# A hybrid decoder layer on one core: weight rows of 512 columns and four accumulators from the second merge branch on

## The chip, the cores and the metric

The kernel runs on one core of one Trainium2 chip. The metric is the device time of one execution in microseconds; the median of three runs is given, and beside it one execution that the hardware profiler recorded.

## The reference

One inference step of a one-layer decoder trunk in float32, for 256 prompt tokens and 8 x 4 sample tokens, T = 288 tokens together, with a model width of 2048.

```python
h = rmsnorm(x, norm_mix)
P = h @ w_in                       # (288 x 2048) @ (2048 x 16416)
y[0], y[1], y[2] = retention(P), gated_deltanet(P), gla(P)      # 1024 wide each
br    = einsum('blnc,ncd->blnd', y, w_branch)                   # three times (1024 x 2048)
gates = sigmoid(mg + b_merge)      # mg: the last 3 * 2048 columns of P
x = x + sum(gates * br, axis=2) @ w_o                           # 2048 x 2048
gate, up = split(rmsnorm(x, norm_ffn) @ w_gate_up, 2)           # 2048 x (2 * 5632)
x = x + (silu(gate) * up) @ w_down                              # 5632 x 2048
y = rmsnorm(x, norm_final)         # and the new states of the three mixers
```

## The kernel before

Activations are kept transposed, 128 channels on the partitions and 288 tokens along the free axis, so a weight block of 128 x 128 is TensorE's stationary operand and the tokens stream past it. Each float32 operand is split into a high part (`xh`, `yh`, `ah`, `m0`; for weights `wh`) and the rest (`xl`, `yl`, `al`, `m1`; `wl`), and a product is the sum of three matmuls: high by high, low activations by high weights, high activations by low weights.

All large products go through `dense` and `products` (lines 324 and 330). One call makes 256 output columns: two accumulators of [128, 288] in two PSUM banks of the pool `pd` (four banks; another four, `pm`, serve the mixers and the transposes). The contraction runs in blocks of 128 rows (k). `load` (line 318) fetches four of them at a time, [128, 4, 256], 512 KB, through SP's DMA queue; the pool `raw` holds four such loads. Two k at a time are split: ACT casts `wh` (line 347), DVE subtracts to get `wl` (line 348, recorded as L131); there are four buffers of each. Then 2 x 2 x 3 matmuls follow (recorded as L125).

The order of work: setup; the mixers, whose projections by `x_in` are interleaved with the mixers' own steps; then three merge branches, `branch(n, order)` (line 1219); `merge_out` (line 1259) with `w_o`; `ffn` (line 1307). A branch loads the eight blocks of its mixer's result from DRAM (`yr` from `ys`, line 1225, two buffers) and splits them into `yh` and `yl` (ACT at L169, DVE at L131). Then it goes over eight groups j of 256 columns. A group first makes the gate logits from columns 10272 + 2048 n + 256 j of `w_in` (16 k, eviction `evg`), then the branch product from `w_branch` (8 k, eviction `evb`). Branch 0 stores its gated product in DRAM (`accd`). Branch 1 loads it again, one `yr` tile for each 128 columns (line 1248), and adds. Branch 2 adds and hands on the split sum `m0`, `m1` (`merged`). `merge_out` loads the residual (`xres` from `xT`, line 1271, three buffers), and starts the first gate product of the feed-forward part early. `ffn` goes over two halves of 22 blocks of 128 hidden columns: for each 256 of them a gate and an up product (16 k each), then eight down products over 22 k. After each of the last eight, the rows are transposed by TensorE (L122), squared by ACT and multiplied by the final norm's gain by DVE.

A Tile scheduler decides the order on each engine's queue; what `tc.high_priority()` encloses (the weight loads and splits) comes early. Queues are in order: an instruction that waits holds up what stands behind it.

Of the kernel before, what the change touches and what calls it, by code (L numbers as in the profile page):

```python
# [10 lines left out]
F32 = mybir.dt.float32  # L11
# [3 lines left out]
ALU = mybir.AluOpType  # L15
# [14 lines left out]
HALF = FFB // 2  # L30
# [24 lines left out]
def shape_consts():  # L55
    """Tables that depend on shapes and positions alone."""
# [42 lines left out]
class Trunk:  # L99
    def __init__(self, ctx, tc, ins, outs):  # L100
        self.ctx, self.tc, self.nc = ctx, tc, tc.nc
        self.i, self.o = ins, outs
        self.uid = 0
        self.active = []

# [50 lines left out]
    def pump(self, part=None):  # L156
        """Emits the next steps of the mixers under way."""
# [15 lines left out]
    def setup(self):  # L173
# [41 lines left out]
        # keeps the tensor engine busy until x is there, for its clock  # L215
# [83 lines left out]
    def rms(self, pool, ssq, tag):  # L299
        """ssq [tokens, group, part] of partial sums of squares -> 1/rms [tokens, group]."""  # L300
# [7 lines left out]
    def rowscale(self, pool, r, tag):  # L308
        """r [tokens, group] on every partition, [P, T]."""
# [63 lines left out]
    def gates(self):  # L373
# [21 lines left out]
        # running sums over time of log-sigmoid of the forget logits  # L395
# [7 lines left out]
    def gate_cols(self, z, bz):  # L403
        """Decay sums and write strengths of the delta rule, by head rows and by token columns."""
# [74 lines left out]
    def gdn_conv(self, pair, part):  # L479
        """One of q, k, v of a pair of heads: projection, convolution, 2*silu -> [P, 2, T]."""  # L480
# [50 lines left out]
    def gated(self, n, c0):  # L531
        """2*silu of a projection of 256 columns -> [P, 2, T]."""
# [11 lines left out]
    def finish(self, tr_ps, gate, gcol, n, blk):  # L544
        """y = transposed output * gate (* gain), kept in DRAM until the branch product."""
# [7 lines left out]
    def gdn_mix(self, pair, qs, ks, vs, szs):  # L553
# [12 lines left out]
        for z in hd:  # L566
            # norms of q and k per token, token-major k and v with their factors
# [40 lines left out]
        # chains of the two heads: prompt chunks [P, 4, P] as (chunk, head), samples [NS, 2, NS]  # L608
# [3 lines left out]
        for hh, z in enumerate(hd):  # L612
            # decays, k k^T and k q^T
# [31 lines left out]
        # inverses of the unit triangular systems (u: transposed) by doubling of the block size: up to 8 with a  # L645
        # block in each partition, up to 32 by the diagonal blocks of 32
# [56 lines left out]
        # blocks of 64  # L703
# [23 lines left out]
        # the whole blocks  # L727
# [16 lines left out]
        # outputs and states  # L744
# [84 lines left out]
    # outer products of the sample states: rows hi, hi, lo of k against hi, lo, hi of v  # L829
# [22 lines left out]
    def diag8(self, t, wide, thin):  # L852
        """Pairs of [72, 8, 8] (heads and chunks by 16 blocks, heads of the samples by 4) and the scratch."""
# [9 lines left out]
    def gdn_setup(self):  # L863
# [7 lines left out]
        # scratch of the diagonal blocks of 8; the second pair stays 0 beside them  # L871
# [20 lines left out]
    def values(self, v):  # L892
        """v: [P, 2, T] of one head -> token-major [P, 2, 256] and [NS, 256]."""
# [128 lines left out]
    def spread(self, h, q, f):  # L1022
        """q * f of the samples, high and low part, masked per batch: [P, NB, 2 NS]."""
# [80 lines left out]
    def gla_logits(self, pair):  # L1104
        """The forget logits of two heads: min(z, 0) and exp(-|z|), [P, 2, T] each."""
# [14 lines left out]
    def gla_head(self, h, q, k, v, sg, b):  # L1120
# [16 lines left out]
        for n, s in enumerate(LEVELS + (128,)):  # L1137
# [18 lines left out]
            if s >= 32:  # L1156
                # only the blocks of the level
# [18 lines left out]
        # decayed q and k of the states  # L1176
# [42 lines left out]
    def branch(self, n, order, emit=None):  # L1219
# [11 lines left out]
        for j in range(D // CHUNK):  # L1231
            th = [self.t(self.bp, (P, T), "bt", bufs=4) for _ in range(2)]

            def evg(m, pp):
                blk = n * KT + 2 * j + m
# [3 lines left out]
            self.x_in(O_MG + n * D + j * CHUNK, evg)  # L1239

            def evb(m, pp):
                k = 2 * j + m
# [11 lines left out]
            self.dense(yh, yl, wb[:, :, j * CHUNK:(j + 1) * CHUNK], 8, evb)  # L1254
# [4 lines left out]
    def merge_out(self, merged, bp):  # L1259
        """x + merged @ w_o, its norm's split operands and 1/rms rows."""  # L1260
# [6 lines left out]
        for j in range(D // CHUNK):  # L1267
            def ev(m, pp):
                k = 2 * j + m
# [14 lines left out]
            self.dense([z[0] for z in merged], [z[1] for z in merged], wo[:, :, j * CHUNK:(j + 1) * CHUNK], KT, ev)  # L1284
# [20 lines left out]
        self.early = self.products(blocks(xh), blocks(xl), wg[:, :, 0:CHUNK], KT, False, norm())  # L1305

    def ffn(self, st):
# [5 lines left out]
        NJ = D // CHUNK  # L1313
# [4 lines left out]
        for half in range(2):  # L1318
# [24 lines left out]
            for j in range(NJ):  # L1343
# [5 lines left out]
                if half == 0:  # L1349
                    continue  # L1350
# [102 lines left out]
```

## Time and profile before

| | us |
|---|---|
| median of three runs (lowest, highest) | 2365.64 (2364.16, 2368.34) |
| span of the profiled execution | 2364.7 |
| median less that span | 0.9 |
| TensorE busy in the span | 2206.0 (93%) |
| VectorE busy | 1363.7 (58%) |
| ScalarE busy | 1023.4 (43%) |
| DMA, mean over the span | 157 GB/s |

The page's first part gives the busy time of each engine, its second the same in 40 slices of the span. Matrix records overlap, since each lasts about 0.3 us while a new one starts every 0.13 us; so the pace of TensorE is read from counts of records in a stretch and not from their durations. In a table by stretches the columns are: the stretch in us from the span's start, its length, then busy time and number of instructions of PE (matmuls), PEld (weight loads), DVE, ACT and POOL, the mean granted TensorE clock (1.00 is 2.4 GHz, 0.50 would be 1.2), the mean busy share of the 16 DMA engines, and GB/s. Records are counted in each stretch that they touch. In the list of waits the columns are who waited for whom, us in total, times, longest. In the chain each row is a start, a duration and what ran or was waited for.

### The profile page before, as it was taken

What the parts mean: (1) busy time and instruction counts of PE and PEld (TensorE: products, weight loads), DVE (VectorE), ACT (ScalarE), POOL (GpSimd) and SP (SyncE); (2) the same over time, 40 slices, a digit from 0 to 9 for tenths busy, and PEclk for the clock granted to TensorE, in tenths of its full rate; (3) what the DMA queues carried; (4) which work ended last, traced back from release to release, by engine and by line L of the source; (5) the groups of instructions that cost most, each with busy time, mean ns of one, the idle gap of its engine ahead of it and who ended that gap; (6) DMA issues with size and microseconds to landing.
All of it is one profiled execution on the core that took longest, in us unless ns stands there. A gap on an engine that the chain in (4) does not pass through costs nothing.

```text
span 2364.7 us, 42849 instructions
## 1 busy us (share of the span) xinstructions
PE 2206.0 (93%) x16476; PEld 2139.8 (90%) x16476; DVE 1363.7 (58%) x2952; ACT 1023.4 (43%) x2138; POOL 209.1 (9%) x264
## 2 busy tenths in 40 slices
PE   8686998996899899989989999999999999999997
PEld 6676898996799899989989999999999999999997
DVE  4554685684478566445445466655555455655554
ACT  4352453453256345334334344444444344444443
POOL 2000230231044124000000000000000000000000
PEclk8797998998899999999999999999999999999999
DMA  8986576588667776888887776655555555555553
GB/s 170 111 113 115 138 195 139 133 160 142 110 142 170 157 157 173 187 149 193 159 148 167 139 179 187 189 162 168 164 167 161 169 168 163 169 162 169 156 159 127
DMA packets 387609, 371.74 MB, mean 157 GB/s; under 512 B 26370, under 2 KB 384860, under 8 KB 387244
## 3 DMA queue, kind: packets, MB, share of 16 engines
q1 hardware_dynamic: 386236, 366.22, 65.9%
q8 instruction: 129, 2.11, 0.4%
q0 software_dynamic: 896, 2.45, 0.3%
q14 instruction: 76, 0.62, 0.1%
q10 hardware_dynamic: 272, 0.34, 0.1%
HBM read 342.02 MB, written 26.92 MB: 156 GB/s over the span
## 4 chain that ended last, share of the span: by engine, by line
PE 75%; DMA 15%; DVE 4%; SPq 2%; ACT 2%; issue 1%; POOL 1%; DVEq 0%; POOLq 0%; ACTq 0%
PE pd L125 69%; DMA raw<-in_w_in_dram 6%; PE pm L125 5%; DMA yr<-ys 2%; DVE wl L131 2%; DMA dgu<-u 1%; PE pm L122 1%; DMA dgb<-bt 1%; DMA srow<-in_state_gdn_conv_dram 1%; DMA s<-in_state_ret_dram 1%; DMA out_dram<-s 1%; ACT wh L347 1%; DMA uc<-dgu 1%; DMA b<-dgbs 1%; DVE r L140 0%
## 5 line engine op out<-in xcount | busy, mean ns | idle before, releaser
L131 DVE TENSOR_TENSOR wl<-raw,wh 128x512 fp32r<-128x512 f32 (+1 forms) x1208 | 847.4, 705 | 788.9 <-ACT wh L347 763.6
L347 ACT CAST wh<-raw 128x512 fp32r<-128x512 f32 x1200 | 738.1, 619 | 1050.8 <-PE pd L125 855.2
L125 PE MATMUL pd<-xh,wh 128*128 128x288 f32 x3472 | 1049.3, 303 | 60.4 <-ACT wh L347 55.8
L125 PE MATMUL pd<-xh,wl 128*128 128x288 f32 x3472 | 1048.3, 304 | 34.7 <-DVE wl L131 34.7
L125 PE MATMUL pd<-xl,wh 128*128 128x288 f32 x3472 | 1048.4, 302 | 0.2 <-DVE xl L140 0.2
L125 PEld LDWEIGHTS pd<-xh,wh 128*128 128x128 f32 x3472 | 671.0, 194 | 69.6 <-ACT wh L347 60.6
L125 PEld LDWEIGHTS pd<-xh,wl 128*128 128x128 f32 x3472 | 669.1, 193 | 44.2 <-DVE wl L131 40.5
L125 PEld LDWEIGHTS pd<-xl,wh 128*128 128x128 f32 x3472 | 670.5, 193 | 3.6 <-issue 1.0
L125 PE MATMUL pd<-ah,wl 128*128 128x288 f32 x704 | 208.0, 295 | 0.0
L125 PE MATMUL pd<-al,wh 128*128 128x288 f32 x704 | 207.8, 295 | 0.0
L125 PE MATMUL pd<-ah,wh 128*128 128x288 f32 x704 | 207.8, 295 | 0.0
L125 PEld LDWEIGHTS pd<-ah,wh 128*128 128x128 f32 x704 | 132.5, 188 | 0.1
L125 PEld LDWEIGHTS pd<-ah,wl 128*128 128x128 f32 x704 | 132.3, 188 | 0.0
L125 PEld LDWEIGHTS pd<-al,wh 128*128 128x128 f32 x704 | 132.1, 188 | 0.0
L125 PE MATMUL pd<-yh,wh 128*128 128x288 f32 x384 | 113.4, 298 | 4.3 <-ACT wh L347 2.8
L125 PE MATMUL pd<-yl,wh 128*128 128x288 f32 x384 | 114.4, 298 | 0.3 <-DVE yl L131 0.3
L125 PE MATMUL pd<-yh,wl 128*128 128x288 f32 x384 | 114.0, 297 | 0.0
L125 PE MATMUL pd<-m,wh 128*128 128x288 f32 x512 | 101.6, 295 | 0.0
L125 PEld LDWEIGHTS pd<-m,wh 128*128 128x128 f32 x512 | 82.1, 188 | 0.0
L125 PEld LDWEIGHTS pd<-yh,wh 128*128 128x128 f32 x384 | 72.5, 190 | 5.6 <-ACT wh L347 3.0
L125 PE MATMUL pd<-m,wl 128*128 128x288 f32 x256 | 75.5, 295 | 0.0
L145 POOL TENSOR_TENSOR fr<-fs,c_mh 128x3 f32<-128x3 f32 x1 | 0.8, 849 | 843.1 <-DVE fs L137 843.1
(336 smaller groups left out, 1827.6 us busy)
## 6 DMA issues: line engine op xcount, KB each, us to landing
raw<-in_w_in_dram SPq DMA_DIRECT2D x252, 512.0 KB
raw<-in_w_gate_up_dram SPq DMA_DIRECT2D x176, 512.0 KB
raw<-in_w_down_dram SPq DMA_DIRECT2D x80, 512.0 KB
raw<-in_w_branch_dram SPq DMA_DIRECT2D x48, 512.0 KB
raw<-in_w_o_dram SPq DMA_DIRECT2D x32, 512.0 KB
out_dram<-s SPq DMA_DIRECT2D x16, 512.0 KB
s<-in_state_gdn_dram SPq DMA_DIRECT2D x8, 512.0 KB
s<-in_state_ret_dram SPq DMA_DIRECT2D x16, 256.0 KB
```

Of the source, the lines that this page charges most:

```text
L122: self.nc.tensor.transpose(out, in_, self.ident[:k, :k])
L125: self.nc.tensor.matmul(out, lhsT=lhsT, rhs=rhs, start=start, stop=stop)
L131: self.nc.vector.tensor_tensor(out, a, b, op=op)
L145: self.nc.gpsimd.tensor_tensor(out, in_, c[:n].to_broadcast(list(in_.shape)), op=ALU.pow)
L347: nc.scalar.copy(h, src)
```

## The change

From branch 1 on, products go through two new functions, `wide` and `products4`: 512 output columns in a call, four accumulators, taken in turn from `pd` and `pm` (four banks each). A load holds two k of 512 columns, [128, 2, 512], the same 512 KB in rows of 2 KB in place of 1 KB; a split handles one k of 512 columns, the same 128 x 512 elements. Mixers and branch 0 keep `dense`. The tiles `bt` get eight buffers, `sg` one of twice the size. The feed-forward part goes over 24 and 20 hidden blocks in place of 22 and 22. The final transposes go to banks of the pool whose group was just emptied, one [128, 512] tile for each group of tokens.

```diff
-HALF = FFB // 2
+PARTS = (24, 20)
+WIDE = 512
...
+    def wide(self, xh, xl, wv, kt, evict):
+        acc, self.early = self.early or self.products4(xh, xl, wv, kt), None
+        pool, tiles = acc
+        for m in range(4):
+            evict(m, tiles[m][:, :T])
+        return pool
+
+    def products4(self, xh, xl, wv, kt, steps=None):
+        nc, tc = self.nc, self.tc
+        pool, tag = ((self.pd, "pd"), (self.pm, "pm"))[self.turn]
+        self.turn = 1 - self.turn
+        acc = [self.t(pool, (P, 512), tag) for _ in range(4)]
+        for k0 in range(0, kt, 2):
+            raw = self.t(self.wp, (P, 2, WIDE), "raw", bufs=4)
+            with tc.high_priority():
+                nc.sync.dma_start(out=raw, in_=wv[:, k0:k0 + 2])
+            for k in range(2):
+                wh = self.t(self.wp, (P, WIDE), "wh", F32R, bufs=4)
+                wl = self.t(self.wp, (P, WIDE), "wl", F32R, bufs=4)
+                with tc.high_priority():
+                    nc.scalar.copy(wh, raw[:, k])
+                    self.tt(wl, raw[:, k], wh.bitcast(F32), ALU.subtract)
+                kk = k0 + k
+                for m in range(4):
+                    ms = slice(m * P, (m + 1) * P)
+                    o = acc[m][:, :T]
+                    self.mm(o, wh[:, ms], xh[kk], kk == 0, False)
+                    self.mm(o, wh[:, ms], xl[kk], False, False)
+                    self.mm(o, wl[:, ms], xh[kk], False, kk == kt - 1)
+            if steps is not None:
+                next(steps)
+        return (pool, tag), acc
...
     def branch(self, n, order, emit=None):
...
-        for j in range(D // CHUNK):
-            th = [self.t(self.bp, (P, T), "bt", bufs=4) for _ in range(2)]
+        W = WIDE if n else CHUNK
+        for j in range(D // W):
+            th = [self.t(self.bp, (P, T), "bt", bufs=8) for _ in range(W // P)]
...
-            self.x_in(O_MG + n * D + j * CHUNK, evg)
+            if n:
+                self.wide(blocks(self.xh), blocks(self.xl), self.w_in(O_MG + n * D + j * W, W), KT, evg)
+            else:
+                self.x_in(O_MG + j * W, evg)
...
-            self.dense(yh, yl, wb[:, :, j * CHUNK:(j + 1) * CHUNK], 8, evb)
+            (self.wide if n else self.dense)(yh, yl, wb[:, :, j * W:(j + 1) * W], 8, evb)
...
     def merge_out(self, merged, bp):
...
-            self.dense([z[0] for z in merged], [z[1] for z in merged], wo[:, :, j * CHUNK:(j + 1) * CHUNK], KT, ev)
+            self.wide([z[0] for z in merged], [z[1] for z in merged], wo[:, :, j * WIDE:(j + 1) * WIDE], KT, ev)
...
     def ffn(self, st):
...
+        b0 = 0
+        for part in PARTS:
             ah, al = [], []
+            for j in range(part // 4):
+                c0 = (b0 + 4 * j) * P
+                sg = self.t(fp, (P, 4, T), "sg", bufs=1)
...
+                pool, tag = self.wide(ah, al, wd[:, b0:b0 + part, j * WIDE:(j + 1) * WIDE], part, evd)
...
                 for g, (t0, w) in enumerate(GROUPS):
-                    src = pa[:, g * CHUNK:(g + 1) * CHUNK] if g < 2 else pb[:NS, :CHUNK]
-                    junk = self.t(fp, (P, CHUNK), "junk", bufs=2)
+                    src = self.t(pool, (P, 512), tag)[:w]
+                    for m in range(4):
+                        self.tr(src[:, m * P:(m + 1) * P], self.x2[4 * j + m][:, t0:t0 + w])
+                    junk = self.t(fp, (P, WIDE), "junk", bufs=2)
                     self.act(junk[:w], src, AF.Square, accum_out=ssq[:w, g, j:j + 1])
                     self.tt(xo[g][:, cs], src, nfb[:w, cs], ALU.mult)
```

Up to branch 1 all queues hold the same instructions in the same order. ACT's queue at the entry of branch 1, after the last evictions of branch 0's gate logits (`bt`), stood before as

```order
L347 CAST wh_12449<-raw_12447 128x512
L169 CAST yh_12403<-yr_12401 128x288
L347 CAST wh_12465<-raw_12447 128x512
L347 CAST wh_12483<-raw_12481 128x512
L169 CAST yh_12409<-yr_12407 128x288
L169 CAST yh_12415<-yr_12413 128x288
L347 CAST wh_12499<-raw_12481 128x512
L347 CAST wh_12517<-raw_12515 128x512
L169 CAST yh_12421<-yr_12419 128x288
L169 CAST yh_12427<-yr_12425 128x288
```

and stands now as

```order
L348 CAST wh_12453<-raw_12451 128x512
L171 CAST yh_12403<-yr_12401 128x288
L348 CAST wh_12469<-raw_12451 128x512
L348 CAST wh_12487<-raw_12485 128x512
L171 CAST yh_12409<-yr_12407 128x288
L171 CAST yh_12415<-yr_12413 128x288
L348 CAST wh_12503<-raw_12485 128x512
L171 CAST yh_12421<-yr_12419 128x288
L171 CAST yh_12427<-yr_12425 128x288
L348 CAST wh_12521<-raw_12519 128x512
```

The casts of the branch's own tiles (`yh`) still stand between those of the first gate weights (`wh`); one weight cast fewer lies between the second and the third pair. A weight cast serves 12 matmuls before and after.

SP's queue at the entry of branch 2 stood before as (`accd` tiles of branch 1's last group, `ys` tiles of branch 2, gate loads from `w_in`)

```order
L1248 DMA yr_14216<-accd_108 128x288
L321 DMA raw_14276<-in_w_in_dram 128x4x256
L321 DMA raw_14310<-in_w_in_dram 128x4x256
L321 DMA raw_14344<-in_w_in_dram 128x4x256
L321 DMA raw_14378<-in_w_in_dram 128x4x256
L321 DMA raw_14418<-in_w_branch_dram 128x4x256
L1225 DMA yr_14224<-ys_107 128x288
L321 DMA raw_14452<-in_w_branch_dram 128x4x256
L1225 DMA yr_14230<-ys_107 128x288
L1225 DMA yr_14236<-ys_107 128x288
```

and stands now as

```order
L343 DMA raw_14382<-in_w_in_dram 128x2x512
L343 DMA raw_14416<-in_w_in_dram 128x2x512
L1289 DMA yr_14212<-accd_108 128x288
L1289 DMA yr_14216<-accd_108 128x288
L343 DMA raw_14450<-in_w_in_dram 128x2x512
L1262 DMA yr_14224<-ys_107 128x288
L1262 DMA yr_14230<-ys_107 128x288
L343 DMA raw_14484<-in_w_in_dram 128x2x512
L1262 DMA yr_14236<-ys_107 128x288
L343 DMA raw_14518<-in_w_in_dram 128x2x512
L1262 DMA yr_14242<-ys_107 128x288
L1262 DMA yr_14248<-ys_107 128x288
```

The last two `accd` tiles of branch 1 moved behind five gate loads of the next group, and the `ys` tiles of branch 2 now stand among the gate loads of its first group, where before they stood behind them and the branch loads.

DVE's queue at a group's end in branch 1, which had two products and two additions, stands now as (`bt` the gated products, `acc` the additions of the `accd` tiles)

```order
L142 SCALAR_TENSOR_TENSOR bt_12888<-bt_12888,pm_13176 128x288
L133 TENSOR_TENSOR acc_12383<-yr_13316,bt_12887 128x288
L142 SCALAR_TENSOR_TENSOR bt_12889<-bt_12889,pm_13177 128x288
L142 SCALAR_TENSOR_TENSOR bt_12890<-bt_12890,pm_13178 128x288
L133 TENSOR_TENSOR acc_12384<-yr_13320,bt_12888 128x288
L133 TENSOR_TENSOR wl_13392<-raw_13373,wh_13391 128x512
L133 TENSOR_TENSOR wl_13410<-raw_13407,wh_13409 128x512
L133 TENSOR_TENSOR acc_12385<-yr_13324,bt_12889 128x288
L133 TENSOR_TENSOR acc_12386<-yr_13328,bt_12890 128x288
L133 TENSOR_TENSOR wl_13426<-raw_13407,wh_13425 128x512
```

Two subtractions lie between the second and the third addition; the tiles `yr` of the third and the fourth take the buffers of the first and the second.

## Rows read from the trace of the kernel before

**Rows 1.** The page, parts 1 and 2: busy time, and 40 slices of the span.

```profile
PE 2206.0 (93%) x16476; PEld 2139.8 (90%) x16476; DVE 1363.7 (58%) x2952; ACT 1023.4 (43%) x2138; POOL 209.1 (9%) x264
...
PE   8686998996899899989989999999999999999997
```

**Rows 2.** Stretches: branch 1, branch 2, output projection, feed-forward part.

```profile
1051.16:1223.96 172.80, 159.07 (x1155) 157.55 (x1153) 85.84 (x148) 67.75 (x118) 0.00 (x0) 0.95 0.81 167
1223.96:1401.09 177.13, 161.89 (x1155) 159.35 (x1154) 92.52 (x168) 74.09 (x135) 0.00 (x0) 0.94 0.78 156
1401.09:1502.63 101.54, 101.54 (x770) 101.54 (x769) 62.64 (x112) 50.51 (x94) 0.00 (x0) 1.00 0.62 185
1502.63:2350.07 847.44, 847.29 (x6389) 846.64 (x6387) 470.78 (x810) 364.10 (x659) 0.85 (x1) 1.00 0.53 163
```

**Rows 3.** Stretches of 10 us in branches 1 and 2.

```profile
1050.00:1060.00 10.00, 6.11 (x46) 5.87 (x45) 0.69 (x1) 0.62 (x1) 0.00 (x0) 1.00 1.03 83
1060.00:1070.00 10.00, 3.69 (x14) 3.34 (x15) 3.54 (x8) 3.02 (x7) 0.00 (x0) 0.55 0.72 183
...
1140.00:1150.00 10.00, 9.74 (x71) 9.27 (x71) 4.05 (x8) 2.28 (x4) 0.00 (x0) 1.00 1.01 83
1150.00:1160.00 10.00, 6.73 (x31) 6.26 (x30) 3.32 (x6) 2.90 (x5) 0.00 (x0) 0.66 0.94 256
...
1230.00:1240.00 10.00, 2.61 (x16) 1.91 (x14) 0.76 (x2) 1.15 (x3) 0.00 (x0) 0.75 0.93 173
1240.00:1250.00 10.00, 8.92 (x48) 8.46 (x48) 4.31 (x8) 3.28 (x7) 0.00 (x0) 0.74 0.76 118
1250.00:1260.00 10.00, 7.13 (x39) 6.67 (x40) 5.91 (x12) 5.75 (x12) 0.00 (x0) 0.83 0.72 179
...
1320.00:1330.00 10.00, 7.22 (x51) 6.52 (x49) 3.24 (x7) 1.92 (x4) 0.00 (x0) 1.00 1.01 124
1330.00:1340.00 10.00, 8.88 (x44) 8.66 (x45) 5.13 (x9) 5.00 (x9) 0.00 (x0) 0.66 0.88 191
```

**Rows 4.** Waits, 1051 to 1401 us: who for whom, us in total, times, longest.

```profile
ACT yh L169 <- DMA yr<-ys: 36.1, 12, 12.5
ACT wh L347 <- DMA raw<-in_w_in_dram: 34.4, 9, 6.0
...
PE pd L125 <- ACT wh L347: 27.2, 7, 9.7
```

**Rows 5.** The chain that ended last, 1040 to 1270 us: start, us, what.

```profile
1047.18 17.27 DMA yr<-ys
...
1135.56 17.94 DMA raw<-in_w_in_dram
...
1247.75 5.83 DMA yr<-ys
...
1254.55 3.66 DMA yr<-ys
```

**Rows 6.** Timeline of SP's queue: start, us from first to last, line, what.

```profile
1036.67 9.93 SPq L321 DMA_DIRECT2D raw<-in_w_in_dram  x4
...
1126.00 9.93 SPq L321 DMA_DIRECT2D raw<-in_w_in_dram  x4
```

**Rows 7.** Timeline of ACT at the entry of branch 1; in brackets the idle time before.

```profile
1064.48 0.76 ACT L169 CAST yh<-yr 128x288 fp32r<-128x288 f32 x2 [12.51 <-DMA yr<-ys]
```

**Rows 8.** Groups by line and shape, 1420 to 2364 us: busy us, mean ns.

```profile
L131 DVE TENSOR_TENSOR wl<-raw,wh 128x512 fp32r<-128x512 f32 x577 | 399.2, 692 | 396.9 <-ACT wh L347 392.0
L347 ACT CAST wh<-raw 128x512 fp32r<-128x512 f32 x577 | 357.1, 619 | 511.1 <-PE pd L125 495.9 <-ACT ah L169 7.7 <-ACT th L128 7.4
...
L140 DVE SCALAR_TENSOR_TENSOR acc<-pd,acc 128x288 f32<-128x288 f32 x32 | 13.7, 457 | 4.8 <-PE pd L125 4.8
```

**Rows 9.** Timeline of the tail, after the last matmul of the down product.

```profile
2350.95 0.38 ACT L128 ACTIVATE junk<-pm 128x256 f32<-128x256 f32 x1 [6.88 <-PE pm L122]
...
2351.46 0.42 DVE L131 TENSOR_TENSOR xo<-pm,nfb 128x256 f32<-128x256 f32 x1 [1.04 <-ACT junk L128]
```

More of the change, by code (lines that the diff above doesn't have):

```diff
@@ L104, in __init__ @@
         self.active = []
+        self.turn = 0
     def nm(self, s):
@@ L1266, in merge_out @@
         wo = self.i["w_o"][0].rearrange("(k p) c -> p k c", p=P)
-        for j in range(D // CHUNK):
+        for j in range(D // WIDE):
             def ev(m, pp):
-                k = 2 * j + m
+                k = 4 * j + m
                 xr = self.t(bp, (P, T), "xres", bufs=3)
@@ L1312, in ffn @@
         xo = [self.t(fp, (w, D), f"xo{g}") for g, (t0, w) in enumerate(GROUPS)]
-        NJ = D // CHUNK
+        NJ = D // WIDE
         ssq = self.t(fp, (P, 3, NJ), "ssq3")
@@ L1317, in ffn @@
         wd = self.i["w_down"][0].rearrange("(k p) c -> p k c", p=P)
-        for half in range(2):
+        b0 = 0
+        for part in PARTS:
             ah, al = [], []
-            for j in range(HALF // 2):
-                c0 = half * HALF * P + j * CHUNK
-                sg = self.t(fp, (P, 2, T), "sg", bufs=2)
+            for j in range(part // 4):
+                c0 = (b0 + 4 * j) * P
+                sg = self.t(fp, (P, 4, T), "sg", bufs=1)
                 def evg(m, pp):
@@ L1339, in evu @@
                     al.append(l)
-                self.dense(blocks(self.xh), blocks(self.xl), wg[:, :, c0:c0 + CHUNK], KT, evg)
-                self.dense(blocks(self.xh), blocks(self.xl), wg[:, :, FF + c0:FF + c0 + CHUNK], KT, evu)
+                self.wide(blocks(self.xh), blocks(self.xl), wg[:, :, c0:c0 + WIDE], KT, evg)
+                self.wide(blocks(self.xh), blocks(self.xl), wg[:, :, FF + c0:FF + c0 + WIDE], KT, evu)
             for j in range(NJ):
                 def evd(m, pp):
-                    a = self.x2[2 * j + m]
+                    a = self.x2[4 * j + m]
                     self.stt(a, pp, 0.5, a, ALU.mult, ALU.add)
-                self.dense(ah, al, wd[:, half * HALF:(half + 1) * HALF, j * CHUNK:(j + 1) * CHUNK], HALF, evd)
-                if half == 0:
+                pool, tag = self.wide(ah, al, wd[:, b0:b0 + part, j * WIDE:(j + 1) * WIDE], part, evd)
+                if b0 == 0:
                     continue
-                cs = slice(j * CHUNK, (j + 1) * CHUNK)
-                pa, pb = self.ps(), self.ps()
-                for m in range(2):
-                    a = self.x2[2 * j + m]
-                    for g in range(2):
-                        self.tr(pa[:, g * CHUNK + m * P:g * CHUNK + (m + 1) * P], a[:, g * P:(g + 1) * P])
-                    self.tr(pb[:NS, m * P:(m + 1) * P], a[:, NPR:])
+                cs = slice(j * WIDE, (j + 1) * WIDE)
                 for g, (t0, w) in enumerate(GROUPS):
-                    src = pa[:, g * CHUNK:(g + 1) * CHUNK] if g < 2 else pb[:NS, :CHUNK]
-                    junk = self.t(fp, (P, CHUNK), "junk", bufs=2)
+                    src = self.t(pool, (P, 512), tag)[:w]
+                    for m in range(4):
+                        self.tr(src[:, m * P:(m + 1) * P], self.x2[4 * j + m][:, t0:t0 + w])
+                    junk = self.t(fp, (P, WIDE), "junk", bufs=2)
                     self.act(junk[:w], src, AF.Square, accum_out=ssq[:w, g, j:j + 1])
                     self.tt(xo[g][:, cs], src, nfb[:w, cs], ALU.mult)
+            b0 += part
         r = self.rms(fp, ssq, "f")
```

10 lines of the change are left out of this document (5 added, 5 removed).

## The prediction

> **What bounds the kernel now.** I read the page's first two parts first [rows 1]. TensorE is busy 93% of the span, and in the second half all slices but two show a 9 in its row: there an engine beside it can only matter where TensorE stops. So the next view is the stages that the change touches [rows 2]: branch 1, branch 2, the output projection, the feed-forward part, the tail. What to see there is how close TensorE is to its own pace in each. The feed-forward stretch holds 6389 matrix records in 847.44 us, that is 132.6 ns each, at clock 1.00 and without idle time; the output projection has 770 in 101.54, 131.9 ns. These two are bound by TensorE alone. The two branch stretches are not. Each is 8 column groups of 16x6 + 8x6 = 144 matmuls, 1152 in all, worth 152.8 us at 132.6 ns, but they take 172.80 and 177.13. **20.0 us are lost in branch 1 and 24.3 us in branch 2**, 44.3 in all, and nothing worth speaking of elsewhere.
>
> Where they are lost is read from slices of 10 us [rows 3]. A full slice counts some 77.5 matmuls (10 us at 132.6 ns are 75.4, and records that reach over an edge count on both sides). The deficits sit at four places. At the entry of branch 1 there are 46 and 14 in two slices (95 missing, 12.6 us, and a few more behind them: 13.0). At 1140 to 1160 there are 71 and 31 (7.0 us). At the entry of branch 2 there are 16, 48 and 39 (129.5 missing, 17.2 us). At 1320 to 1340 there are 51 and 44 (8.0 us). Scaled to what branch 2 loses, its two places are 16.6 and 7.7. Part of each is not idleness but the half clock behind it (mean granted clock 0.55 and 0.66 in the slices after the stop, so partly at 1.2 GHz).
>
> What releases TensorE there: ACT's casts of the weights, 27.2 us [rows 4], and those wait for DMAs, 34.4 us for w_in and 36.1 us for the ys tiles (yr). The chain names single transfers of 17.94 us (a w_in load) and 17.27 us (a yr load that stands behind such loads) [rows 5]. Around them the DMA engines are full (share 1.01 to 1.03) and move only 83 GB/s; ten microseconds later they move 183 and 256 at a smaller share [rows 3]. So these loads are slow in themselves, not late.
>
> Which loads? SP issues four w_in loads in a row just before branch 1 (1036.67), and the four of 1126.00 come 89.3 us later [rows 6]: four groups of 144 x 0.1326 = 19.1 us and the 13.0 lost at the entry. They are the gate columns of j = 0 and j = 4; the places in branch 2 fit the same two. A gate group starts at byte 41,088 + 8192n + 1024j of a 65,664-byte row of w_in, so the slow kilobyte comes once in every 4 KB. At 83 GB/s a load of 524,288 bytes takes 6.3 us; TensorE uses one up in 24 matmuls, 3.18 us. Four slow loads are 4 x 3.12 = 12.5 us late together, of which TensorE lost 7.0 at 1140 to 1160: the buffers absorbed **5.5 us**.
>
> **The change part by part.** *TensorE:* the same number of matmuls and weight loads; one load still feeds 24 matmuls (2 x 4 x 3 in place of 4 x 2 x 3). Nothing, at either clock. *ACT and DVE:* as many casts (619 ns) and subtractions (692 ns) of the same 128x512 size [rows 8], nothing. *PSUM:* a group's four banks are emptied under the next group, which runs 96 to 288 matmuls, 12.7 us or more, against four evictions of about 0.46 us for each DVE operation [rows 8]; covered. *Output projection and feed-forward:* no idle time now, so longer rows can give nothing there. A shorter DMA time is hidden by TensorE.
>
> *The gate loads.* A row is now 2 KB, its first half from the slow kilobyte in groups 0 and 2 of each branch, its second half from a fast one. Eight such loads follow each other in place of four. What one takes, no row shows. From below: if the fast half rides beside the slow one, the slow half alone sets it, 3.15 us. From above: if the whole row runs at the slow pace, 6.3. One after the other the halves take 3.15 + 1.0 (256 GB/s in 1150 to 1160) = 4.2. I take **3.7**, between riding and adding: the 16 DMA engines work on different rows, and in the slow slices they are at full share with few bytes moved, so much of their time looks like waiting that another row's fast half could fill. Eight loads are then 8 x 0.5 = 4.2 us late, under the 5.5 that the buffers absorb, so the two places in mid-branch (7.0 and 7.7) go to 0 (2.5 each at 4.2).
>
> *The entries.* ACT stands at the cast of the third yr tile from 1052 to 1064.48 [rows 7], because that tile queued behind four slow loads. With 3.7 in place of 6.3 it lands some 10 us earlier, near 1054; TensorE, three casts ahead (36 matmuls from 1051.16), ran dry at about 1055.9, so the first stop nearly goes. But the order now puts a slow load before each further pair of yr tiles, which have two buffers: some 4 us for each pair, while ACT hands TensorE one or three casts (1.6 us of matmuls each) between pairs. I keep 4 us of the 13.0. At the entry of branch 2 the yr casts now come eight casts into a gate group of 16, each pair followed by two casts: 3 us of 16.6 stay. Bounds 0 and all.
>
> *New waits.* The third and fourth accd tiles of a group in branch 1, and the fourth residual tile in the projection, are issued only when the first ones are used. SP then stands for one eviction with five of the next group's loads already issued, and DVE may stand for one transfer (3.66 us for a yr load that is not held up [rows 5]). The casts run up to four ahead, 6.4 us of TensorE, and cover that; uncovered it would be 8 times 3.66 to 5.83 us. I take 0.
>
> *Tail.* After the last matmul ACT squares and DVE multiplies pieces of 512 in place of 256 columns (now 0.38 and 0.42 us [rows 9]); the chain of three grows by about 0.7. Each of the three earlier sets of 12 transposes may wait 0.2 us. Together +1.3.
>
> **Sum:** -(13.0 - 4) - 7.0 - (16.6 - 3) - 7.7 + 1.3 = -36.0. The profiled execution's span is 2364.7, so 2328.7; the median of the runs, 2365.64, stands 0.9 above the span, which gives **2329.6, say 2330 us**.
>
> The Trainium skill has a rule that speaks against this edit (DMA: Bandwidth & Descriptors, "Latency and other measured facts"): HBM rows at a pitch near a large power of two alias on memory channels, and what helps is another pitch; it adds that a pitch padded by 192 bytes stayed slow. The pitch here is 64 KiB + 128 bytes before and after. The trace agrees in so far as strided loads keep the DMA engines full at a quarter of the rate reached elsewhere; no run yet shows another row length.
>
> **The rivals.** *Halves add up.* The slow kilobytes stay as slow as they are, and the fast ones come on top: 4.2 us a load. Eight are 8 us late, 2.5 lost at each mid place, and the entries keep 7 and 6: 18 lost, 2341. That is what the skill's rule would make of it. For it: the slow slices' DMA engines are at their full share, so nothing seems free to overlap [rows 3].
>
> *The yr pairs set the entries.* If the two-buffer round trips, not the slow loads, cost the entries (after 1241 further yr loads stand on the chain, two of them at 5.83 and 3.66 us, with no slow load left before them [rows 5]), 13.0 and 16.6 stay and only 14.7 goes: 2352.
>
> *Slower: the whole 2 KB row runs at the slow pace.* Place: the eight gate loads of groups 0 and 2. Price: 8 x 3.12 = 25 us late, less 5.5, 19.5 at each of four places, 78 against 44.3 now: +35 with the tail, 2401. It decides from 5.2 us a load on (10.75 lost at each place). Against it: the group after a slow one was always fast, so the neighbouring kilobyte is not slow by itself.
>
> *Slower: the new waits are not covered.* Eight group ends at 5.83 us would cost 47, more than the gain: 2376.
>
> *Nothing happens* (loads change, the stops only move): 2365.
>
> **How the numbers follow.** Forecast (2322 to 2338) 0.52; halves add up 0.18; yr pairs 0.11; whole rows slow 0.10; waits uncovered 0.04; nothing 0.05. The range goes from 2320 (all 44.3 gone, 2321, and a little) to 2357 (the yr rival with the tail), and leaves out 0.19. The forecast's own range is 2322 to 2338. A measurement of this kernel tells 0.2%, 4.7 us, from no change. Faster 0.81, the same 0.05, slower 0.14.
>
> **What would show it.** Right: branch 1 takes some 157 us and branch 2 some 156, with slices of 75 to 78 matmuls throughout; the w_in stretches of groups 0 and 2 run at 130 to 170 GB/s; ACT's wait for w_in falls from 34.4 us to under 10; the feed-forward stretch keeps 132.6 ns a matmul; the tail is 15 to 16 us. Wrong in size: 110 to 125 GB/s there, and short stops in mid-branch (halves add up), or yr waits of 20 us or more (pairs). Wrong in sign: still 83 GB/s for 50 us at a time, or DVE standing at the accd additions at each group's end. If the feed-forward stretch changes by more than 5 us, I have missed something about TensorE itself.

## The result and the profile after

| | before | after |
|---|---|---|
| median of the runs shown with the result (lowest, highest), us | 2364.9 (2362.15, 2368.34) | 2325.16 (2316.99, 2326.31) |
| ratio, with its 95% interval | | 0.9821 (0.9801, 0.9841) |
| span of the profiled execution, us | 2364.7 | 2324.2 |

The changed kernel is faster by some 40 us. The forecast was 2330 in a range of 2320 to 2357. First the page of the changed kernel, busy time and the row of TensorE in 40 slices [rows 1]:

```profile
PE 2193.6 (94%) x16476; PEld 2131.1 (92%) x16476; DVE 1350.2 (58%) x2940; ACT 1027.2 (44%) x2114; POOL 209.5 (9%) x264
...
PE   8686998998699899999999999999999999999997
```

From the fifteenth slice (813 us) on, and so in both branches, the row has nothing but 9 up to the tail. The view by stretches (columns as in [rows 2]: branch 1, branch 2, output projection, feed-forward part, tail) says what each gave:

```profile
1054.52:1207.47 152.95, 152.91 (x1154) 152.68 (x1153) 83.38 (x146) 68.07 (x118) 0.00 (x0) 1.00 0.66 186
1207.47:1362.18 154.71, 153.70 (x1155) 152.77 (x1154) 89.69 (x166) 72.77 (x132) 0.00 (x0) 1.00 0.62 173
1362.18:1464.14 101.96, 101.96 (x771) 101.96 (x770) 61.03 (x113) 50.64 (x94) 0.00 (x0) 1.00 0.60 183
1464.14:2308.83 844.69, 844.69 (x6384) 844.30 (x6383) 461.54 (x803) 367.29 (x639) 0.85 (x1) 1.00 0.55 164
2308.83:2324.20 15.37, 1.47 (x14) 1.15 (x12) 5.50 (x11) 4.01 (x8) 0.85 (x1) 0.68 0.44 154
```

Against [rows 2], branch 1 lost 19.85 us, branch 2 22.42, the feed-forward part 2.75; the projection took 0.42 longer and the tail 0.74 (14.63 before). Branch 1 begins 3.36 us later than before, after code that is the same. The sum is -40.5 us, which is the difference of the two spans. At 152.8 us for 1152 matmuls, branch 1 now runs at TensorE's own pace and branch 2 is 1.9 us above it.

The slices of 10 us at three of the four places of [rows 3]: entry of branch 1, middle of branch 1, entry of branch 2:

```profile
1050.00:1060.00 10.00, 10.00 (x78) 10.00 (x77) 5.52 (x11) 3.86 (x9) 0.00 (x0) 1.00 0.77 210
1060.00:1070.00 10.00, 9.96 (x75) 9.73 (x74) 6.52 (x12) 6.12 (x12) 0.00 (x0) 1.00 0.85 199
...
1130.00:1140.00 10.00, 10.00 (x77) 10.00 (x77) 7.09 (x15) 3.96 (x7) 0.00 (x0) 1.00 0.82 200
1140.00:1150.00 10.00, 10.00 (x78) 10.00 (x77) 4.62 (x7) 3.72 (x6) 0.00 (x0) 1.00 0.82 190
...
1220.00:1230.00 10.00, 9.19 (x65) 8.42 (x63) 4.71 (x10) 4.21 (x10) 0.00 (x0) 1.00 0.76 202
1230.00:1240.00 10.00, 9.80 (x74) 9.63 (x73) 7.31 (x14) 6.27 (x14) 0.00 (x0) 1.00 0.68 208
```

Where 83 GB/s stood at a DMA share of 1.01 to 1.03, there are now 190 to 210 at 0.68 to 0.85, and the counts are full but for 2.5 matmuls at the entry of branch 1 and 12.5 and 3.5 at that of branch 2. The granted clock stays at 1.00, so the half clock behind the stops went with them. The list of waits of the two branches (1054 to 1362 us) holds, of the lines of [rows 4]:

```profile
ACT yh L171 <- DMA yr<-ys: 18.4, 9, 3.6
...
DVE acc L133 <- DMA yr<-accd: 3.4, 5, 0.8
ACT wh L348 <- DMA raw<-in_w_in_dram: 1.4, 1, 1.4
...
PE pd L127 <- ACT wh L348: 0.6, 2, 0.5
```

The wait for gate weights fell from 34.4 us to 1.4 and TensorE's for ACT's casts from 27.2 to 0.6. ACT still waits 18.4 us for the ys tiles, but nearly all of it under TensorE's work.

### The profile page after: what moved, and what is told of

The parts are those of the page before. It is cut to its first block, busy times and chain, and to the rows that moved or that the text cites. A ratio compares the mean times of both kernels' runs of the same rounds, so it can differ in the third digit from the quotient of the medians.

```text
span 2324.2 us, 42820 instructions
## 1 busy us (share of the span) xinstructions
PE 2193.6 (94%) x16476; PEld 2131.1 (92%) x16476; DVE 1350.2 (58%) x2940; ACT 1027.2 (44%) x2114; POOL 209.5 (9%) x264
## 4 chain that ended last, share of the span: by engine, by line
PE 80%; DMA 13%; DVE 3%; SPq 1%; ACT 1%; issue 1%; POOL 0%; POOLq 0%; DVEq 0%; ACTq 0%
PE pd L127 49%; PE pm L127 30%; DMA raw<-in_w_in_dram 5%; DMA dgu<-u 1%; PE pm L124 1%; DMA dgb<-bt 1%; DMA srow<-in_state_gdn_conv_dram 1%; DMA yr<-ys 1%; DVE wl L133 1%; DMA s<-in_state_ret_dram 1%; DMA out_dram<-s 1%; DMA uc<-dgu 1%; DMA b<-dgbs 1%; DMA ev<-fsum 0%; SPq L706 0%
## 5 line engine op out<-in xcount | busy, mean ns | idle before, releaser
L127 PE MATMUL pd<-xh,wh 128*128 128x288 f32 x2768 | 838.1, 304 | 37.5 <-ACT wh L384 33.1
L127 PE MATMUL pd<-xh,wl 128*128 128x288 f32 x2768 | 832.0, 304 | 34.0 <-DVE wl L133 33.9
L127 PE MATMUL pd<-xl,wh 128*128 128x288 f32 x2768 | 836.2, 303 | 0.2 <-DVE xl L142 0.2
L127 PEld LDWEIGHTS pd<-xh,wh 128*128 128x128 f32 x2768 | 535.0, 194 | 46.1 <-ACT wh L384 36.5
L127 PEld LDWEIGHTS pd<-xh,wl 128*128 128x128 f32 x2768 | 532.4, 194 | 42.1 <-DVE wl L133 38.5
L127 PEld LDWEIGHTS pd<-xl,wh 128*128 128x128 f32 x2768 | 535.6, 194 | 3.9 <-issue 1.0
L127 PE MATMUL pm<-xh,wl 128*128 128x288 f32 x704 | 207.8, 295 | 0.0
L127 PE MATMUL pm<-xl,wh 128*128 128x288 f32 x704 | 207.3, 294 | 0.0
L127 PE MATMUL pm<-xh,wh 128*128 128x288 f32 x704 | 207.0, 294 | 0.0
L127 PEld LDWEIGHTS pm<-xh,wl 128*128 128x128 f32 x704 | 132.1, 188 | 0.0
```

Of the source, the lines that this page charges most:

```text
L127: self.nc.tensor.matmul(out, lhsT=lhsT, rhs=rhs, start=start, stop=stop)
```

## The experiments

The change alters row length, the number of accumulators and the size of a split all at once, so the first question was which of them did it. A "slow load" below is one of gate columns j = 0 or j = 4.

**The price of a load with nothing beside it.** Seventeen sets of eight loads (512 KB each, four in flight) stand behind the end of the changed kernel:

```diff
+    def probe(self):
...
+        for n, f in enumerate(modes):
+            for z in range(8):
+                src, sh = f(z)
+                raw = self.t(pp, (P, 1024), "pr", bufs=4)
...
+                nc.sync.dma_start(out=out, in_=src)
```

> The changed kernel, with 17 sets of 8 loads of 512 KB behind its end, whose data nobody uses; four are in flight at a time, so the spacing of the landings is the price of a load with nothing beside it. Theory 1 (a slow kilobyte whose rows wait, so that another row's fast half fills the time): rows of 1 KB at gate column group j = 0 and j = 4 take about 6.3 us a load, at j = 1, 2, 3 2.0 to 3.2; rows of 2 KB take 3.1 to 3.4 at j = 0 and at j = 3 (whose second half is slow), about 2.5 at j = 1 and 2; 1 KB loads of j = 0 and j = 1 in turn take as long on the mean as the 2 KB rows. Theory 2 (row length itself: a short row has a price of its own): the 1 KB loads in turn take 4.2 or more on the mean while the 2 KB rows take 3.2. Theory 3 (halves add up): both 4.2. Pitch between the partitions of one load: if that is what makes the kilobyte slow, loads that give each partition 4 (or 16) neighbouring rows of w_in take under 3.2 us at j = 0 too; if it is the address alone, they stay at 6.3. w_gate_up: 2.0 to 3.2 in rows of 1 KB and of 2 KB.

The stretches inside the sets, in order: rows of 1 KB at j = 0, at j = 4; rows of 2 KB at j = 0, at j = 1, at j = 3; 1 KB loads of j = 0 and j = 1 in turn; rows of 4 KB from j = 0; 1 KB at j = 0 with 16 and with 4 neighbouring rows in a partition; w_gate_up in rows of 1 KB. The last two columns are the DMA engines' share and GB/s:

```profile
2330.00:2370.00 40.00, 0.00 (x0) 0.00 (x0) 1.08 (x7) 0.00 (x0) 0.00 (x0) 0.50 0.79 89
...
2450.00:2485.00 35.00, 0.00 (x0) 0.00 (x0) 0.92 (x6) 0.00 (x0) 0.00 (x0) 0.50 0.79 88
2492.00:2509.00 17.00, 0.00 (x0) 0.00 (x0) 0.92 (x6) 0.00 (x0) 0.00 (x0) 0.50 0.93 185
2513.00:2523.00 10.00, 0.00 (x0) 0.00 (x0) 0.92 (x6) 0.00 (x0) 0.00 (x0) 0.50 0.97 302
...
2540.00:2557.00 17.00, 0.00 (x0) 0.00 (x0) 0.80 (x6) 0.00 (x0) 0.00 (x0) 0.50 1.02 171
2562.00:2580.00 18.00, 0.00 (x0) 0.00 (x0) 0.92 (x6) 0.00 (x0) 0.00 (x0) 0.50 0.92 166
2586.00:2594.00 8.00, 0.00 (x0) 0.00 (x0) 0.93 (x6) 0.00 (x0) 0.00 (x0) 0.50 0.84 310
2600.00:2640.00 40.00, 0.00 (x0) 0.00 (x0) 0.92 (x6) 0.00 (x0) 0.00 (x0) 0.50 0.80 80
2675.00:2712.00 37.00, 0.00 (x0) 0.00 (x0) 0.92 (x6) 0.00 (x0) 0.00 (x0) 0.50 0.82 88
2745.00:2753.00 8.00, 0.00 (x0) 0.00 (x0) 0.77 (x5) 0.00 (x0) 0.00 (x0) 0.50 1.03 333
```

Divide GB/s by the bytes of a row. At j = 0, 89 GB/s in rows of 1 KB are 87 rows a microsecond; 185 in rows of 2 KB are 90; 310 in rows of 4 KB are 76, but that stretch is 8 us long and its engines are not full (0.84), so it says least. **A row that touches the slow kilobyte has a price of its own, some 11 to 12 ns, whatever it carries besides.** It need not start there: rows of 2 KB at j = 3, whose second half is slow, run at 171. Fast rows beside slow ones are free: j = 0 and j = 1 in turn move 166 GB/s, nearly as the 2 KB rows do. So a load of 2 KB rows takes 524,288 B / 185 GB/s = 2.8 us and not 4.2; "halves add up" falls. Whether the partitions of a load lie 65,664, 262,656 or 1,050,624 bytes apart makes little difference (89, 88, 80), so the place within a row of w_in decides, not the step between partitions. One figure does not fit what was expected: rows of 1 KB alone moved 174 and 185 GB/s at j = 2 and 3, but only 120 at j = 1, 4.4 us a load in place of 3.2 or less; why is open.

**Row length undone.** Each gate load of the branches is two transfers with rows of 1 KB:

```diff
-                nc.sync.dma_start(out=raw, in_=wv[:, k0:k0 + 2])
+                    for h in range(2):
+                        nc.sync.dma_start(out=raw[:, :, h * CHUNK:(h + 1) * CHUNK], in_=wv[h][:, k0:k0 + 2])
```

> The changed kernel, but each gate load of branches 1 and 2 is made of two transfers with rows of 1 KB, one for each half of the 512 columns. Theory 1 (what counts is that slow and fast kilobytes are in flight together): as the change, 2325 to 2328, no stop in mid-branch. Theory 2 (row length): slow and fast half one after the other, 4.2 us a pair, some 2.5 us lost at each of the two places in mid-branch and 3 to 6 at each entry, 2335 to 2341; at the worst all of it is back, 2360.

Measured: 2326.41 us, 0.9834 (0.9787, 0.9881), branches of 155.90 and 154.66 us. Rows of 2 KB are not needed; that the slow kilobyte and a fast one are in flight together is enough.

**Two slow kilobytes in one call.** The columns of a call are the groups j and j + 4, those of w_branch too, each half a transfer with rows of 1 KB:

```diff
-                self.wide(blocks(self.xh), blocks(self.xl), self.w_in(O_MG + n * D + j * W, W), KT, evg)
+                self.wide(blocks(self.xh), blocks(self.xl), [self.w_in(O_MG + n * D + c * CHUNK) for c in (j, j + 4)], KT, evg)
```

> The changed kernel with other columns in a call: 512 columns are the groups of 256 numbered j and j + 4 (two transfers with rows of 1 KB each), so that both slow kilobytes of a branch meet in its first call; four accumulators, order and bytes stay. Theory 1 (the slow kilobyte, wherever it is): the first call of each branch has 8 loads of 6.3 us in a row where TensorE wants 3.2, 25 us late less the 5.5 that the buffers absorb, so 19 to 25 us lost at each entry, nothing in mid-branch: 2363 to 2375. Rival (the four accumulators over eight banks made the gain): 2325 to 2330.

Measured: 2325.3 us, 0.9841 (0.9785, 0.9897), branches of 156.19 and 154.89 us. **Theory 1 fell by 38 us**: two slow kilobytes do not hurt each other. Either the four accumulators did the work after all, or transfers of two k are not slow, or j = 0 and j = 4 are slow at different places. The next runs were made to part these.

**Which loads share a place.** A second set of loads behind the kernel, and the kernel before with each load cut in two transfers of two k:

```diff
+        mode(8, 128, [G])
+        mode(4, 256, [G, G + 1024])
+        mode(4, 256, [G, G + 2048])
+        mode(4, 256, [G - 32])
+        mode(4, 256, [G + 64])
...
+            for q in range(0, kn, 2):
+                e = min(q + 2, kn)
+                self.nc.sync.dma_start(out=raw[:, q:e], in_=src[:, q:e])
```

> The changed kernel with 15 further sets of loads behind its end (4 MB each, 2 MB in flight, data that nobody uses), to find why two slow kilobytes in one call (slow_pairs, 2325 us) cost nothing. Theory P (one kilobyte column of w_in is served by something that gives some 90 GB/s, and another kilobyte, slow alone or not, by something else): rows of 1 KB at j = 0 take 5.7 us for 512 KB whatever the size of the transfer (4, 2 or 1 k), j = 0 and j = 4 in turn take 2.9 on the mean, j = 0 and j = 8 too. Theory T (size of the transfer: two k in one transfer are not slow, four are): j = 0 with 2 k in a transfer takes 3.2 or less, j = 0 and j = 4 in turn with four k stay at 5.7. Rows of 512 bytes: 5.7 or more by both. Rows that start 128 bytes ahead of j = 0, 256 or 512 bytes behind it: 5.7 if the place modulo 4 KB need not be exact, falling towards 2.9 where the row reaches into the next kilobyte.

The sets are not issued in the order of the program, and some overlap; each stretch lies where its own set moves the data, or all but a little of it. In order: one k in a transfer at j = 0; rows of 512 bytes at j = 0; two k in a transfer at j = 0; j = 0 and j = 4 in turn; j = 0 and j = 8 in turn; rows that start 128 bytes ahead of j = 0, and 256 bytes behind it; rows that start at the first byte of a row of w_in:

```profile
2397.00:2414.00 17.00, 0.00 (x0) 0.00 (x0) 0.00 (x0) 0.00 (x0) 0.00 (x0) 0.50 0.89 88
2422.00:2455.00 33.00, 0.00 (x0) 0.00 (x0) 0.00 (x0) 0.00 (x0) 0.00 (x0) 0.50 0.68 48
2462.00:2482.00 20.00, 0.00 (x0) 0.00 (x0) 0.92 (x6) 0.00 (x0) 0.00 (x0) 0.50 0.78 88
...
2570.00:2588.00 18.00, 0.00 (x0) 0.00 (x0) 0.77 (x5) 0.00 (x0) 0.00 (x0) 0.50 0.91 168
...
2640.00:2660.00 20.00, 0.00 (x0) 0.00 (x0) 0.46 (x3) 0.00 (x0) 0.00 (x0) 0.50 1.02 86
2664.00:2684.00 20.00, 0.00 (x0) 0.00 (x0) 0.97 (x9) 0.00 (x0) 0.00 (x0) 0.50 0.97 84
...
2730.00:2750.00 20.00, 0.00 (x0) 0.00 (x0) 0.77 (x5) 0.00 (x0) 0.00 (x0) 0.50 0.89 148
...
2784.00:2824.00 40.00, 0.00 (x0) 0.00 (x0) 1.08 (x7) 0.00 (x0) 0.00 (x0) 0.50 0.85 85
```

The size of a transfer does not matter (88 and 88; theory T falls). Rows of 512 bytes make 48 GB/s, again 94 rows a microsecond, where "5.7 or more" was expected without a reason: bytes are not what is paid for. j = 0 and j = 4, 4096 bytes apart, move 168 in turn, j = 0 and j = 8, 8192 bytes apart, only 86, where theory P had expected 2.9 us a load as well and 6.1 came. The first byte of a row (85 GB/s) and byte 16,384 (86) are slow too. So, as far as it was tried, there are two such places in every 8 KB of a row of w_in, each serves 80 to 94 rows a microsecond, and they serve side by side. From 256 bytes behind j = 0 on, a row of 1 KB no longer pays the full price (148).

> The kernel before, but each weight load of four k is made of two transfers of two k; rows of 1 KB, two accumulators and all else stay. Theory P: the four slow loads in a row stay at 6.3 us, 2360 to 2370. Theory T: the stops in the branches go, 2328 to 2335, and those of the mixers' slow groups become shorter too, so possibly below 2320.

Measured: 2362.64 us, 1.0003 (0.9989, 1.0016): the stops stay, as by theory P.

**The same place in both halves.** If that is right, a call of four accumulators must be slow again when both its halves visit one place. The second half comes from the other branch's gate columns:

```diff
+                self.wide(blocks(self.xh), blocks(self.xl), [self.w_in(O_MG + b * D + j * CHUNK) for b in (n, 3 - n)], KT, evg)
```

> As slow_pairs, but the two halves of a gate call of branch n are group j of branch n and group j of the other branch, 8192 bytes apart in a row of w_in (half of the gate logits are so taken from the other branch's columns; the work is as much). Theory P (rows that touch the same place in 8 KB are served one after the other, some 88 a us, whatever their length): both halves of the first call are at the one place, 512 rows for 512 KB, 5.9 us a load where TensorE wants 3.2; 8 loads are 22 us late, less the 5.5 that the buffers absorb, so some 16 us lost at each entry, none in mid-branch: 2325 + 33 = 2358 (2350 to 2370), with the DMA engines full at 83 to 95 GB/s there. Rival (four accumulators, or transfers of two k, are what keeps the loads up with TensorE): 2321 to 2330, as slow_pairs.

Measured: 2362.07 us, 0.9989 (0.997, 1.0008). Its two branches, and two slices at the entry of the first:

```profile
1050.94:1223.68 172.74, 157.03 (x1155) 155.76 (x1153) 82.73 (x146) 67.88 (x118) 0.00 (x0) 0.96 0.79 166
1223.68:1400.80 177.12, 160.24 (x1154) 157.78 (x1153) 89.91 (x166) 72.61 (x132) 0.00 (x0) 0.94 0.79 157
```

```profile
1046.00:1056.00 10.00, 7.48 (x57) 7.25 (x55) 2.90 (x5) 2.54 (x6) 0.00 (x0) 1.00 0.68 86
1056.00:1066.00 10.00, 1.63 (x7) 1.63 (x8) 2.16 (x5) 1.38 (x3) 0.00 (x0) 0.58 0.97 113
```

172.74 and 177.12 us are the lengths of before, 172.80 and 177.13 [rows 2]; that they agree to a tenth is chance, since here the first call of a branch loses it all, and before there were two places. This kernel differs from rows1k only in which columns a gate call takes, and it gives back all that the branches gained. **Four accumulators over eight banks do not bring the gain by themselves; where a call's rows lie decides it.** Two accumulators with mixed rows were not run in branches 1 and 2; early_loads, below, is the nearest case, in branch 0.

**The change in the branches alone**, with projection and feed-forward part as before:

> The change in branches 1 and 2 alone; output projection and feed-forward part as before. Theory (all of the gain is in the gate loads of the branches, but for the 2.7 us that the feed-forward stretch lost, 847.4 to 844.7): 2327 to 2328.5, feed-forward stretch 847 again, tail 14.6. Rival (longer rows or four accumulators are worth something wherever they are used): over 2335, and the branches not at 153 and 155.

```profile
1046.79:1201.51 154.72, 152.91 (x1155) 152.68 (x1153) 83.56 (x146) 68.25 (x118) 0.00 (x0) 1.00 0.67 183
1201.51:1356.26 154.75, 153.68 (x1154) 152.76 (x1153) 89.70 (x166) 72.81 (x132) 0.00 (x0) 1.00 0.63 174
1356.26:1457.81 101.55, 101.55 (x770) 101.55 (x769) 64.37 (x118) 51.19 (x96) 0.00 (x0) 1.00 0.60 185
1457.81:2304.94 847.13, 847.13 (x6389) 846.64 (x6387) 470.62 (x809) 364.09 (x659) 0.85 (x1) 1.00 0.53 163
```

Measured: 2331.25 us, 0.9847 (0.9798, 0.9895). The median is above the 2327 to 2328.5 expected, but the runs spread from 2321.69 to 2335.03. The stretches are the surer reading: the branches have their gain, the feed-forward part is back at 847.1 and the projection at 101.55 (the 101.54 of before). So the 2.4 to 2.8 us of the feed-forward part belong to its wide form.

**What is left.** Branch 0 keeps rows of 1 KB, and the group j = 4 stops TensorE there. If slow rows are free beside others, half of that group can be fetched among the loads of the two groups before it:

```diff
+                self.tile = self.t(self.bp, (P, 4, CHUNK), "early", bufs=2)
...
+                nc.sync.dma_start(out=self.tile[:, ks], in_=self.w_in(O_MG + 4 * CHUNK)[:, 2 * z:2 * z + 2])
...
+                if j == 4:
+                    self.ahead = early[::2]
```

> The changed kernel, and branch 0, which still loads rows of 1 KB, gets the first half of its slow column group (j = 4) in four transfers of 256 KB among the loads of the two groups before it, into two buffers of their own. Theory P: slow rows cost nothing as long as other places are in flight beside them, so the stop of branch 0 at that group (8.5 us in the changed kernel) goes to 2 or less and nothing else moves: 6 us off, 2319 where the changed kernel has 2325. Rival (the slow rows hold up what stands behind them in the queue, so the stop only moves to the groups before): 2323 to 2327, with a stop of 5 us or more at group 2 or 3.

Measured: 2315.91 us, 0.9807 (0.9779, 0.9834). To compare it with the changed kernel on one chip, both ran again, with a third kernel beside them:

> The changed kernel as it is, beside the next two on one chip: 0.982 of the kernel before, 2322 to 2328.

> The kernel of early_loads again, beside the changed kernel on one chip. Theory P: the stop of branch 0 at its slow column group is gone in every execution, 6 to 8 us below the changed kernel. Rival (the 2315.9 of early_loads is the chip or the spread of the mixers' part, which differs by up to 10 us from run to run): within 3 us of it.

Measured: 2323.29 us, 0.9833 (0.9813, 0.9854), and 2314.17 us, 0.9794 (0.9775, 0.9812). The medians are 9.1 us apart, the intervals just clear of each other. The place, first in the changed kernel, then with the early loads:

```profile
970.00:980.00 10.00, 7.26 (x53) 6.80 (x52) 2.20 (x5) 1.97 (x4) 0.00 (x0) 1.00 1.02 100
980.00:990.00 10.00, 5.88 (x36) 5.16 (x37) 3.50 (x6) 2.59 (x5) 0.00 (x0) 0.95 0.86 210
990.00:1000.00 10.00, 10.00 (x69) 10.00 (x68) 5.50 (x11) 4.58 (x8) 0.00 (x0) 0.88 0.82 175
```

```profile
960.00:970.00 10.00, 10.00 (x78) 10.00 (x77) 6.15 (x12) 5.01 (x9) 0.00 (x0) 1.00 1.03 92
970.00:980.00 10.00, 10.00 (x78) 10.00 (x77) 4.56 (x7) 3.71 (x6) 0.00 (x0) 1.00 1.04 270
980.00:990.00 10.00, 10.00 (x77) 10.00 (x76) 6.07 (x11) 4.58 (x8) 0.00 (x0) 1.00 0.85 183
990.00:1000.00 10.00, 10.00 (x78) 10.00 (x77) 4.15 (x6) 4.05 (x7) 0.00 (x0) 1.00 0.67 188
```

53, 36 and 69 matmuls against some 77.5 a slice are 74.5 missing, 9.9 us at 132.6 ns; with the early loads none is missing. **This version is faster than both kernels.** But theory P of early_loads, that slow rows cost nothing beside others, is not what the slices show: from 960 to 970 us the engines still stand full at 92 GB/s, and TensorE runs on, half of the group having come before. An earlier start, two more buffers and mixed rows were changed at once here, and what each gave is open. The third kernel gives the yr tiles four buffers, those loaded from ys and, in branch 1, those from accd:

```diff
-            yr = self.t(self.bp, (P, T), "yr", bufs=2)
+            yr = self.t(self.bp, (P, T), "yr", bufs=4)
```

> early_again with four buffers in place of two for the tiles of the branches' own inputs (yr). Theory (the 2.0 and 1.2 us that the entries of branches 1 and 2 still lose are round trips of pairs of yr tiles): both entries lose under 0.5, branches of 152.7 us each, 2 to 3 us below early_again. Rival (what is left at the entries is the slow rows of the first call, which now have more yr loads among them): the entries lose as much or more, no gain.

```profile
1048.17:1201.23 153.06, 152.93 (x1155) 152.69 (x1154) 82.63 (x144) 67.66 (x116) 0.00 (x0) 1.00 0.68 185
1201.23:1353.90 152.67, 152.67 (x1155) 152.66 (x1154) 89.62 (x166) 73.00 (x132) 0.00 (x0) 1.00 0.64 174
```

Measured: 2317.73 us, 0.98 (0.9782, 0.9818). Both branches are at TensorE's pace, where early_again has 155.06 and 154.57, so the last 2 us of each entry were waits for the two yr buffers. At the entry of branch 2 one load of branch 1's accd tiles stands in that chain ahead of the ys pairs (2.81 us in early_again). The whole is not shorter: the part before branch 1 took 1048.17 us here and 1045.79 there, and a gain of 4 us in two stretches is less than that part varies.

**A fifth weight buffer**, paid for with a fourth of the split buffers:

```diff
-        raw = self.t(self.wp, (P, 4, CHUNK), "raw", bufs=4)
+        raw = self.t(self.wp, (P, 4, CHUNK), "raw", bufs=5)
...
-                wh = self.t(self.wp, (P, 2, CHUNK), "wh", F32R, bufs=4)
+                wh = self.t(self.wp, (P, 2, CHUNK), "wh", F32R, bufs=3)
```

> The changed kernel with five weight buffers in place of four, paid for by three in place of four of each split (wh, wl). Theory P: each of the mixers' stretches of slow loads, and there are some eight with stops of 5 to 17 us, gets 2.6 to 3.1 us more cover: 10 to 20 us off, 2305 to 2315. Rival (TensorE lives on the splits that are done ahead, and three are too few where ACT and DVE also serve the mixers): over 2325.

Measured: 2328.15 us, 0.9859 (0.9834, 0.9884); the part before branch 1 took 1060.08 us where the changed kernel has 1054.52 and 1056.49. No gain, and the rival's figure. The two edits were made together, so whether the fifth buffer gave nothing or the third splits took it back stays open, and with it how much of the mixers' stops comes from slow rows.

## Why the prediction was right

*What bounds the kernel.* That 44.3 us were lost in branches 1 and 2, and that nothing was to be had in the stages behind them, held to 3 us. Ahead of them there was more of the same kind: branch 0 lost 9.9 us at its group j = 4. That the loads were slow in themselves and not late is what the loads behind the kernel show: 5.9 us for 512 KB (89 GB/s) with nothing beside them, 6.3 in the kernel.

*The gate loads, taken at 3.7 us between 3.15 and 6.3.* The mechanism was right, the term too large: 2.8 us, under the lower end too. That end halved the 6.3 us read in the kernel; alone a load of 1 KB rows takes 5.9, and half as many rows, 256 at 90 a microsecond, take 2.8. The slow groups' slices in the changed kernel say the same, 190 to 210 GB/s or 2.5 to 2.8 us a load, above the 130 to 170 GB/s that were to show the forecast right. At 2.8 against the 3.18 that TensorE needs, these loads are never late, so the middles went to 0 as forecast, and "eight loads are 4.2 us late" was not so. The 5.5 us that the buffers were to absorb took all of the 7.0 us lost in mid-branch as lateness; by [rows 3] TensorE was busy for 9.74 and 6.73 us of the two slices, so it stood for some 3.5, and the rest was the half clock. With loads that are not late this did no harm. "Halves add up" (2341) and "the whole 2 KB row runs at the slow pace" (2401) needed 4.2 and 5.2 us.

*The entries, 4 of 13.0 and 3 of 16.6 kept.* Branch 1 keeps 0.15 us and branch 2 1.9 in this profile, 1.7 and 2.1 (154.47 and 154.88 less 152.8) in the second run of the same kernel. What is kept is what the prediction said, round trips through the two yr buffers, as early_yr4 shows. Its price was too high, some 1.5 times what came in branch 2 and more than twice in branch 1: ACT still waited 18.4 us for ys tiles, but 3.6 at most at a time, and TensorE only 0.6 for ACT's casts. As a rival that keeps all of 29.6 us the pairs were wrong.

*Nothing for TensorE, PSUM, ACT and DVE.* In the branches same_place agrees: without the addresses the rest of the change gained nothing. In the feed-forward part it failed, by a little: 844.69 us where it had 847.44, and 844.69 again in rows1k, against 847.13 in branches_only. By the starts of the matmul records, 1.0 us of the 2.75 lies at the transposes (three sets of 12 in the stretch in place of seven of 6) and 1.7 in the spacing of the other matmuls, 132.57 ns in place of 132.87. The projection goes the other way, from 101.54 to 101.96. What in the wide form moves the spacing is not settled.

*New waits, 0.* DVE stood 3.4 us in all for the accd tiles, 0.8 at most, and TensorE not at all for it. At the entry of branch 2, though, one accd load (2.98 us) stands ahead of the ys pairs in the chain that ended last, so the 1.9 us kept there are in part this term. *Tail, +0.7:* 14.63 to 15.37. The +0.6 for the earlier transposes did not come: they took 1.0 us less.

*The sum.* -36.0 was forecast, -40.5 came: branches -42.3 in place of -37.3, feed-forward part and projection -2.3 in place of +0.6, tail +0.7 as said, and +3.4 in the unchanged part before branch 1. That part ended between 1046.5 and 1058.4 us in the profiles of the kernels here that share its code, so nothing says that the change is the reason for it. Without it the sum would have been -43.9, 7.9 us from the forecast in place of 4.5; that much of the nearness is luck.

The Trainium skill's rule (DMA: Bandwidth & Descriptors, "Latency and other measured facts"), that a row pitch at a large power of two is slow and a small pad does not help, has its slow figures from pitches of 2 MiB and more, says nothing of other row lengths than 16 KiB, and calls its mechanism, aliasing of memory channels, an inference. That it would leave the halves to add up was the prediction's reading. The runs fit it in so far as w_gate_up, with a pitch of 45,056 bytes, moves 333 GB/s in rows of 1 KB; but they tried one place there, and at the pitch of w_in most places are fast. They differ in the cure: with the pitch as it was, longer rows, or rows of another place in flight beside, took the stops away, and the measurement decides. Nothing here shows what the two places are.

## What to carry to other kernels

When DMA engines are full and bytes are few, count rows, not bytes, and ask which rows visit the same place: measure one set of loads at a time behind the kernel's end. Where slow rows bunch up, make them longer, or mix them with rows from elsewhere; a stop that four buffers cannot cover can be covered by an early start of part of the loads. A mechanism in a table of stretches is tested best by the kernel that keeps everything of the change but the suspected part: rows1k and same_place differ by an address and by 36 us.

## What the runs showed of the hardware that was not expected

- Rows of w_in (65,664 bytes apart) that touch one place in 8 KB are served at 86 to 94 a microsecond in lengths of 512 bytes, 1 KB and 2 KB (48, 88, 185 GB/s); rows that touch two places 4096 bytes apart run at twice that (168 GB/s in rows of 1 KB).
- The step between the partitions of a load (1, 4 or 16 rows) changes this little (89, 88, 80 GB/s).
- The wide feed-forward part repeats to 0.1 us from kernel to kernel (844.69 in the profiles of after, after_again and rows1k), while the same code before branch 1 varies by 12 us (1046.5 to 1058.4); so small terms are read from stretches and not from medians.
